# The conditioning sums of the mixing, added by accumulating transfers instead of GpSimd

## The chip, the cores and the metric

The kernel runs on one core of a Trainium2 chip, with one launch. The metric is device time in microseconds, the median over runs. The engines go by the profile's names: TensorE (PE, with PEld for its weight loads), VectorE (DVE), ScalarE (ACT), GpSimd (POOL) and SyncE (SP, which only issues DMAs). Each engine takes its own instructions in the order in which they stand in its queue.

## The reference

One decoder layer, 512 tokens of width 2048, in float32. A conditioning vector `c` gives six vectors by one product with `w_ada` (2048 x 12288): shifts, scales and gates around the mixing (`_m`) and around the MLP (`_f`).

```python
c_act = jax.nn.silu(c)
mod = c_act @ w_ada[l] + b_ada[l]
sh_m, sc_m, gt_m, sh_f, sc_f, gt_f = jnp.split(mod[:, None, :], N_MOD, axis=-1)
h = rmsnorm(x, pre_mix_norm[l]) * (1.0 + sc_m) + sh_m
proj = h @ w_in[l]
o_hg = hgrn2_group(proj[..., :HG_COLS], lb_all[l], hg_norm[l])       # 8 heads
o_gdn = gdn_group(proj[..., HG_COLS:], gdn_conv_w[l], ...)           # 8 heads
y = jnp.concatenate([o_hg, o_gdn], axis=-1) @ w_out[l]
x = x + gt_m * rmsnorm(y, post_mix_norm[l])
h = rmsnorm(x, pre_ffn_norm[l]) * (1.0 + sc_f) + sh_f
y = jnp.square(jax.nn.relu(h @ w_ff1[l])) @ w_ff2[l]
x = x + gt_f * rmsnorm(y, post_ffn_norm[l])
```

The change touches how `sc_f`, `sh_f` and `gt_m` (segments 4, 3 and 2 of `mod`) are summed.

## The kernel before, in words

*Stages.* Until about 288 us the kernel computes `sh_m` and `sc_m`, the normed input and the first projections. From 288 to about 1060 us it runs the **mixing**: 16 heads (8 HGRN2, 8 Gated DeltaNet) whose recurrences are many small dependent steps on VectorE, ScalarE, GpSimd and TensorE, and between them, as filling for TensorE, the projections of the heads to come. From 1060 to about 1280 us follow the output product and the residual, then the MLP until the end.

*Products.* A float32 product is made from three products of split operands (`mm3`). Each weight block of 128x1024 is loaded by SP (`raw`), rounded to its upper part on ScalarE (`wh`, L247), and the rest is taken on VectorE (`wl`, L249). In the mixing `WeightStream.get` hands out such a block for each half of a projection (`pj`), and a raw tile has three buffers.

*Conditioning in the mixing.* Segments 4, 3 and 2 of `w_ada` are read as 3 x 4 x 16 = 192 chunks of 128x512: segment, column block `cb` of 512 columns, row block `r`. A chunk is loaded by SP into an `ada` tile (L469, seven buffers, LOOK = 6 chunks ahead), scaled by ScalarE with the 128 values of `c` for its row block (L487), and added by GpSimd into the sum `aacc` of its column block (L489); the first chunk of a column block is scaled straight into `aacc`. So 180 chunks are added and 12 are not. All 16 row blocks of a column block follow each other, then comes the next column block. Five chunks after a column block's last chunk, `finish` sums the 128 partitions on TensorE (`column_sum`, `pca`) and VectorE puts the result into `sc1f` or `shf`; for segment 2 the bias is added on GpSimd (L1310) and the sum is kept for a product with ones (`pgw`) at the end of the mixing. The sums lie in a pool of six buffers (`part`), which they share with six blocks of the first projections. Segment 5 is summed in the same way, after the mixing (`ada_gtf`, `aaccf`).

*What sets the order.* The orders of TensorE and SP in the mixing are the program's own: a list of threads (`run`) yields in turn, by a clock that counts the matmuls' modelled time. ScalarE, VectorE and GpSimd are put in order by the scheduler of the framework, which also places every wait. Chunks are paced by `on_get`: with each weight block handed out, so many chunks are issued that 192 of them would be through after 84 blocks. Their scaling is put behind the last cast of `wh` (`ws.cast`). On GpSimd the sums stand in one queue with steps of the heads: the powers that make a reciprocal root (L465), the masks (`rsm` L1029, `at` L1098) and small memsets.

*Accumulating transfers* are in the kernel already: in the MLP GpSimd issues DMAs that add a weight quarter from DRAM to a tile in SBUF (`raw` L264, 128x1024), and two near the end add one SBUF tile to another (`add_far`).

Of the kernel before, what the change touches and what calls it, by code (L numbers as in the profile page):

```python
# [13 lines left out]
ALU = mybir.AluOpType  # L14
# [16 lines left out]
NV = 1  # L31
PJ = 3
LOOK = 6
T = 512
D = 2048
KT = D // P
NCH = T // P
NH = 8
# [83 lines left out]
def first_sums(key, t, quarter):  # L122

    c, d, e, f = ((key, q, t) for q in ("11", "22", "12", "n"))
    return ([(c, quarter("11", t)), (d, quarter("22", t)), (e, quarter("12", t))],
            [("pool", e, d, e), ("pool", f, c, e)])
# [168 lines left out]
def hybrid_layer_kernel(  # L295
# [7 lines left out]
    nc = tc.nc  # L303
# [53 lines left out]
    l2, s2 = first_sums(jobs[0][0], 0, jobs[0][2])  # L357
# [5 lines left out]
    def bank(tag, name):  # L363
        return psx.tile([P, T], F32, tag=tag, name=name, bufs={"pj": PJ, "wg": 5 - PJ}.get(tag, 1))

# [17 lines left out]
    ws = WeightStream(nc, wpool, plan, 3, 1, (3, 2, 2, 3))  # L383
# [54 lines left out]

    hH = big.tile([P, KT, T], F32R, tag="hH", name="hH")
    hL = big.tile([P, KT, T], F32R, tag="hL", name="hL")  # L440

# [25 lines left out]
    def ada_load(alloc, seg, cb, r):  # L467
        a = alloc(f"ada{seg}_{cb}_{r}")
        nc.sync.dma_start(out=a, in_=w_ada[2 * len(SLOTS) + (ADA_REST.index(seg) * 4 + cb) * KT + r])  # L469
        return a  # L470
# [6 lines left out]
            else:  # L477
                nc.vector.scalar_tensor_tensor(out=acc, in0=av, scalar=cv, in1=acc, op0=ALU.mult, op1=ALU.add)  # L478

    def ada_pool(a, ncol, r0, nr, acc, first, behind=None):  # L480
        if behind is not None:
            with tc.issue_after(behind):
                return ada_pool(a, ncol, r0, nr, acc, first)
        dst = acc if first else a
        for r in range(nr):
            s = slice(r * ncol, (r + 1) * ncol)
            nc.scalar.activation(out=dst[:, s], in_=a[:, s], func=AF.Copy, scale=c2[:, r0 + r : r0 + r + 1])  # L487
        if not first:
            nc.gpsimd.tensor_tensor(out=acc, in0=a, in1=acc, op=ALU.add)  # L489

    def column_sum(ps, i, a, w, start=True, stop=True):
        for g in range(2):
            s = slice(64 * g, 64 * (g + 1))
            mm(ps[s, i, : w.shape[1]], a[:, s], w, start, stop, cost=0.08)
# [20 lines left out]

    def mt(tag, name, bufs=1, shape=(P, T), dt=F32):
        pool = mixA if tag in MIXA else pools["mix"]
        return pool.tile(list(shape), dt, tag=tag, name=name, bufs=bufs)
# [3 lines left out]
    def conv_silu(u, blk, tag, name, bufs):  # L522
        up = mt("up", f"up{name}", 1, (P, T + 3))
        nc.gpsimd.memset(up[:, :3], 0.0)
        nc.scalar.copy(out=up[:, 3:], in_=u)
        z = mt("z", f"z{name}")
        nc.scalar.activation(out=z, in_=u, func=AF.Copy, scale=convT[:, 72 + blk : 73 + blk])
        for j in range(3):
            nc.vector.scalar_tensor_tensor(out=z, in0=up[:, j : j + T],
                                           scalar=convT[:, j * 24 + blk : j * 24 + blk + 1],  # L530
                                           in1=z, op0=ALU.mult, op1=ALU.add)
        th = mt("th", f"th{name}")
        nc.scalar.activation(out=th, in_=z, func=AF.Tanh, scale=0.5)
        dst = mt(tag, name, bufs)
        nc.vector.scalar_tensor_tensor(out=dst, in0=th, scalar=1.0, in1=z, op0=ALU.add, op1=ALU.mult)
        return dst
# [285 lines left out]
    def ada_thread():  # L822
        nl = 0
        for i, (g, j) in enumerate(SLOTS):
# [26 lines left out]
            if g < NV:  # L851
                ada_vector(t[1], w, nr * j, nr, sums[g][1][:, :w], j == 0)
            else:
                ada_pool(t[1], w, nr * j, nr, sums[g][1], j == 0)
# [436 lines left out]
    def ada_tile(name):  # L1291
        return part_pool.tile([P, T], F32, tag="part", bufs=6, name=name)

    def ada_chunks():
        for seg in (4, 3, 2):
            for cb in range(4):
                for r in range(KT):
                    yield seg, cb, r

    def ada_rest():  # L1300
        todo = list(ada_chunks())
        tiles = {}
        accs_ = {}
        late = []

        def finish(seg, cb, acc):
            if seg == 2:
                bgt = ada_tile(f"bgt{cb}")[0:1, :]
                nc.sync.dma_start(out=bgt, in_=b_ada[:, 2 * D + cb * 512 : 2 * D + (cb + 1) * 512])
                nc.gpsimd.tensor_tensor(out=acc[0:1, :], in0=acc[0:1, :], in1=bgt, op=ALU.add)  # L1310
                gacc.append(acc)
                return
            dst, bias = (sc1f, b_scf) if seg == 4 else (shf, b_shf)
            pc = bank("sh", f"pca{seg}_{cb}").rearrange("p (k n) -> p k n", n=64)
            for k in range(4):
                column_sum(pc, k, acc[:, k * P : (k + 1) * P], ones[:, :64])
            ks = slice(4 * cb, 4 * cb + 4)
            nc.vector.tensor_tensor(out=dst[:, ks], in0=pc[:, 0:4, 0], in1=bias[:, ks], op=ALU.add)
            if seg == 4:
                nc.vector.tensor_tensor(out=dst[:, ks], in0=dst[:, ks], in1=w_pf[:, ks], op=ALU.mult)  # L1320

        for i, (seg, cb, r) in enumerate(todo):
            for s2, c2_, r2 in todo[i : i + LOOK]:
                if (s2, c2_, r2) not in tiles:
                    if r2 == 0:
                        accs_[(s2, c2_)] = ada_tile(f"aacc{s2}_{c2_}")
                    tiles[(s2, c2_, r2)] = ada_load(
                        lambda n: ada_pool_.tile([P, T], F32, tag="ada", bufs=LOOK + 1, name=n),
                        s2, c2_, r2)
            acc = accs_[(seg, cb)]  # L1330
            ada_pool(tiles.pop((seg, cb, r)), 512, r, 1, acc, r == 0, ws.cast)
            if late and i >= late[0][0]:
                finish(*late.pop(0)[1:])
            if r == KT - 1:
                late.append((i + 5, seg, cb, acc))
            yield
        for e in late:
            finish(*e[1:])
# [4 lines left out]
    def ada_gtf():  # L1343
# [16 lines left out]

        for i in range(len(seq) + LOOK + 7):
            if i < len(seq):
                queue.append(ada_load(lambda n: ada_pool_.tile([P, T], F32, tag="ada", bufs=LOOK + 1, name=n),
                                      5, *seq[i]))
            if queue and i >= LOOK:
                cb, r = seq[i - LOOK]
                if r == 0:
                    acc = ada_tile(f"aaccf{cb}")
                ada_pool(queue.pop(0), 512, r, 1, acc, r == 0, ws.cast)
                if r == KT - 1:  # L1370
                    bgt = ada_tile(f"bgf{cb}")[0:1, :]
                    nc.sync.dma_start(out=bgt, in_=b_ada[:, 5 * D + cb * 512 : 5 * D + (cb + 1) * 512])
                    nc.gpsimd.tensor_tensor(out=acc[0:1, :], in0=acc[0:1, :], in1=bgt, op=ALU.add)
                    late.append((i + 6, lambda cb=cb, acc=acc: parts(cb, acc)))
            if late and i >= late[0][0]:
                got = late.pop(0)[1]()
                if got is not None:
                    late.append((i + 8, lambda got=got: finish(*got)))
            yield
        for e in late:  # L1380
            e[1]()

    gsteps = ada_gtf()
    steps = ada_rest()
    pace = {"on": False, "n": 0, "done": 0}
    total = sum(1 for e in plan if e[0][0] == "in1") - 12

    def on_get():
        if not pace["on"]:
            return  # L1390
        pace["n"] += 1
        while pace["done"] * total < pace["n"] * 192:
            pace["done"] += 1
            next(steps, None)

# [136 lines left out]
    with ExitStack() as st:  # L1532
# [41 lines left out]
        for nb in range(1, 4):  # L1574
            ps4 = [bank("pj", f"pout{nb}_{tok}") for tok in range(3)] + [bank("sg", f"pout{nb}_3")]
            n = 8 if nb < 3 else 8 - NLAST
# [494 lines left out]
```

## Time and profile before

| | us |
|---|---|
| median of 3 runs | 2559.31 (2556.16 to 2559.85) |
| profiled execution | 2558.09 |
| its span, first to last instruction | 2556.2 |
| TensorE busy in the span | 2427.4 (95%) |
| VectorE busy | 1959.9 (77%) |
| ScalarE busy | 1264.3 (49%) |
| GpSimd busy | 992.9 (39%) |
| mean granted TensorE clock | 0.983 |

The profile is of one execution; times within it count from the first instruction. "Busy" is the union of an engine's instructions, and a matmul's end is modelled. A row of the waits reads: who waited, at which line, on what; us in total, times, longest. A row of a tile reads: line, engine, operation, out<-in, count; shortest/median/longest ns, first and last start. A row of the timeline: start, us, engine, line, operation, and in brackets the idle time before it and what ended it. The page's "PEclk" is the clock that the throttle granted to TensorE, as a share of full speed.

### The profile page before, as it was taken

The page shows a single profiled execution, that of the slowest core. Times are in us where ns is not written, and L with a number is a line of the kernel's source. Part 1 is how long each engine was busy: PE and PEld are TensorE (multiplying, and loading weights), DVE is VectorE, ACT ScalarE, POOL GpSimd, SP SyncE. Part 2 cuts the span into 40 slices and gives each one's busy share as a digit, 9 for nine tenths or more (in the row PEclk, how much of TensorE's full clock was granted, in tenths as well). Part 3 has the DMA queues.
Part 4 walks back from the last instruction along what each step waited for, and adds up shares of the span by engine and source line. Part 5 has one row for each costly group of instructions (what it writes and reads, how often), then busy time and mean ns, then how long its engine had stood idle before and what let it go on. Part 6 is the DMA issues. An engine that isn't in the chain of part 4 may idle for free.

```text
span 2556.2 us, 39334 instructions
## 1 busy us (share of the span) xinstructions
PE 2427.4 (95%) x14763; PEld 2065.9 (81%) x14763; DVE 1959.9 (77%) x2615; ACT 1264.3 (49%) x2012; POOL 992.9 (39%) x720
## 2 busy tenths in 40 slices
PE   5889999998999899999899999999999999999997
PEld 3667777777777778778779999999998888888886
DVE  7997887768595866654687777878788788888887
ACT  5554444444444443465555565656665433333333
POOL 4561244545454541186231222212235244244343
PEclk8999999999999999999999999999999999999999
DMA  8762434444445442476458887888889988988876
GB/s 312 256 211 78 130 121 132 138 156 131 155 147 158 139 146 75 136 264 226 165 173 252 242 273 238 245 253 237 273 249 301 287 252 246 287 258 244 265 211 192
DMA packets 202899, 527.18 MB, mean 206 GB/s; under 512 B 19026, under 2 KB 23492, under 8 KB 202068
## 3 DMA queue, kind: packets, MB, share of 16 engines
q1 hardware_dynamic: 183792, 457.49, 51.6%
q0 software_dynamic: 18144, 66.07, 14.1%
q8 instruction: 116, 1.90, 0.3%
q10 hardware_dynamic: 772, 1.11, 0.1%
q14 instruction: 75, 0.61, 0.1%
HBM read 460.08 MB, written 63.46 MB: 205 GB/s over the span
## 4 chain that ended last, share of the span: by engine, by line
PE 63%; DVE 6%; ACT 2%; issue 2%; POOL 2%; DMA 1%; POOLq 0%; DVEq 0%; SPq 0%; ACTq 0%
PE qx L369 13%; PE px L369 13%; PE pj L369 10%; PE py L369 7%; PE qy L369 6%; PE pout L369 4%; PE pz L369 3%; PE qz L369 3%; DVE wl L249 1%; POOL aaccf L489 1%; PE pa L369 1%; DMA raw<-in_w_ff_dram 0%; DVE uc L1070 0%; PE p L369 0%; DVE utmp L1068 0%
## 5 line engine op out<-in xcount | busy, mean ns | idle before, releaser
L249 DVE TENSOR_TENSOR wl<-raw,wh 128x1024 fp32r<-128x1024 f32 x457 | 701.8, 1541 | 215.2 <-ACT wh L247 214.0
L247 ACT CAST wh<-raw 128x1024 fp32r<-128x1024 f32 x463 | 485.4, 1049 | 625.8 <-PE pj L369 172.1
L489 POOL TENSOR_TENSOR aacc<-ada,aacc 128x512 f32<-128x512 f32 x180 | 270.4, 1503 | 257.3 <-ACT ada L487 249.9
L369 PE MATMUL pj<-hH,wh 128*128 128x512 f32 x768 | 325.6, 424 | 0.0
L369 PE MATMUL pj<-hH,wl 128*128 128x512 f32 x768 | 305.4, 398 | 3.6 <-DVE wl L249 3.6
L369 PE MATMUL pj<-hL,wh 128*128 128x512 f32 x768 | 303.9, 396 | 0.0
L264 POOL DMA_DIRECT2D raw<-in_w_ff_dram x92 | 80.9, 879 | 527.8 <-DVE wl L249 425.3
L269 POOL TENSOR_TENSOR raw<-raw,raw 128x1024 f32<-128x1024 f32 x54 | 161.4, 2989 | 126.5 <-DVE wl L249 68.2
L369 PEld LDWEIGHTS pj<-hH,wl 128*128 128x128 f32 x768 | 146.3, 191 | 38.8 <-DVE wl L249 5.7
L369 PEld LDWEIGHTS pj<-hH,wh 128*128 128x128 f32 x768 | 147.4, 192 | 29.0
L369 PEld LDWEIGHTS pj<-hL,wh 128*128 128x128 f32 x768 | 147.5, 192 | 23.6
L487 ACT ACTIVATE ada<-ada,c 128x512 f32<-128x512 f32 x240 | 160.6, 715 | 0.7 <-DMA ada<-in_w_ada_dram 0.7
L369 PE MATMUL px<-hA,wl 128*128 128x256 f32 x480 | 135.9, 283 | 2.3 <-DVE wl L249 2.3
L249 DVE TENSOR_TENSOR w<-raw,w 128x1024 fp32r<-128x1024 f32 x59 | 116.8, 1992 | 26.5 <-ACT w L247 26.5
L369 PE MATMUL px<-hB,wh 128*128 128x256 f32 x480 | 135.8, 283 | 0.0
L369 PE MATMUL px<-hA,wh 128*128 128x256 f32 x480 | 135.8, 283 | 0.0
L489 POOL TENSOR_TENSOR aaccf<-ada,aaccf 128x512 f32<-128x512 f32 x60 | 99.1, 1652 | 43.0 <-ACT ada L487 38.1
L478 DVE SCALAR_TENSOR_TENSOR asum<-adas,c,asum 128x256 f32<-128x256 f32 (+1 forms) x150 | 105.8, 716 | 2.7 <-DMA adas<-in_w_ada_dram 0.2
L369 PE MATMUL pout<-wh,oH 128*128 128x512 f32 x256 | 101.9, 400 | 3.7 <-ACT wh L247 2.2
L247 ACT CAST w<-raw 128x1024 fp32r<-128x1024 f32 x59 | 61.9, 1049 | 87.6 <-PE qx L369 43.6
L369 PE MATMUL pout<-wl,oH 128*128 128x512 f32 x256 | 100.6, 394 | 1.1 <-DVE wl L249 1.1
L369 PE MATMUL pout<-wh,oL 128*128 128x512 f32 x256 | 100.8, 394 | 0.6 <-DVE oL L1505 0.6
(565 smaller groups left out, 6740.2 us busy)
## 6 DMA issues: line engine op xcount, KB each, us to landing
raw<-in_w_ff_dram SPq DMA_DIRECT2D x233, 512.0 KB, 4.6
raw<-in_w_in_dram SPq DMA_DIRECT2D x128, 512.0 KB, 3.7
ada<-in_w_ada_dram SPq DMA_DIRECT2D x256, 256.0 KB, 3.4
raw<-in_w_ff_dram POOLq DMA_DIRECT2D x92, 512.0 KB, 5.9
adas<-in_w_ada_dram SPq DMA_DIRECT2D x128, 256.0 KB, 4.6
gd<-Y SPq DMA_DIRECT2D x30, 1024.0 KB
hA<-gd SPq DMA_DIRECT2D x47, 512.0 KB, 8.2
hB<-gd SPq DMA_DIRECT2D x47, 512.0 KB, 8.1
```

The source lines that it names most:

```text
L247: self.cast = self.nc.scalar.copy(out=h, in_=raw).ins
L249: eng.tensor_tensor(out=lo, in0=raw, in1=h.bitcast(F32), op=ALU.subtract)
L264: self.nc.gpsimd.dma_start(out=o, in_=src[0], accum_op=ALU.add)
L269: eng.tensor_tensor(out=o, in0=self.raw[src[-1]], in1=self.raw[src[0]], op=ALU.add)
L369: nc.tensor.matmul(ps, lhsT=lhsT, rhs=rhs, start=start, stop=stop, skip_group_check=chain)
L478: nc.vector.scalar_tensor_tensor(out=acc, in0=av, scalar=cv, in1=acc, op0=ALU.mult, op1=ALU.add)
L487: nc.scalar.activation(out=dst[:, s], in_=a[:, s], func=AF.Copy, scale=c2[:, r0 + r : r0 + r + 1])
L489: nc.gpsimd.tensor_tensor(out=acc, in0=a, in1=acc, op=ALU.add)
```

## The change

Five things change, all of them in the mixing. The 180 sums are no longer a GpSimd instruction with two inputs: GpSimd issues a DMA that reads the scaled chunk from SBUF and adds it to `aacc` in SBUF (`accum_op=ALU.add`, through the new argument `far`). The row blocks become the outer loop and the four column blocks the inner one, so that four sums are open at a time and two transfers into the same sum lie four chunks apart. Chunks are loaded 4 ahead (LOOK1) instead of 6, with seven buffers as before. A sum's tile is taken when its first chunk is scaled instead of when it is loaded. The pace goes from 192 to 198. Segment 5 keeps its GpSimd sums. Lines behind the change have numbers that are higher by 1 to 5 in the changed kernel (L469 is L470, L489 is L494, the transfer is L492, L465 is L466).

```diff
+LOOK1 = 4
...
-    def ada_pool(a, ncol, r0, nr, acc, first, behind=None):
+    def ada_pool(a, ncol, r0, nr, acc, first, behind=None, far=False):
         if behind is not None:
             with tc.issue_after(behind):
-                return ada_pool(a, ncol, r0, nr, acc, first)
+                return ada_pool(a, ncol, r0, nr, acc, first, None, far)
         dst = acc if first else a
         for r in range(nr):
             s = slice(r * ncol, (r + 1) * ncol)
             nc.scalar.activation(out=dst[:, s], in_=a[:, s], func=AF.Copy, scale=c2[:, r0 + r : r0 + r + 1])
-        if not first:
+        if first:
+            return
+        if far:
+            nc.gpsimd.dma_start(out=acc, in_=a, accum_op=ALU.add)
+        else:
             nc.gpsimd.tensor_tensor(out=acc, in0=a, in1=acc, op=ALU.add)
...
         for seg in (4, 3, 2):
-            for cb in range(4):
-                for r in range(KT):
+            for r in range(KT):
+                for cb in range(4):
                     yield seg, cb, r
...
-            for s2, c2_, r2 in todo[i : i + LOOK]:
+            for s2, c2_, r2 in todo[i : i + LOOK1]:
                 if (s2, c2_, r2) not in tiles:
-                    if r2 == 0:
-                        accs_[(s2, c2_)] = ada_tile(f"aacc{s2}_{c2_}")
                     tiles[(s2, c2_, r2)] = ada_load(
                         lambda n: ada_pool_.tile([P, T], F32, tag="ada", bufs=LOOK + 1, name=n),
                         s2, c2_, r2)
+            if r == 0:
+                accs_[(seg, cb)] = ada_tile(f"aacc{seg}_{cb}")
             acc = accs_[(seg, cb)]
-            ada_pool(tiles.pop((seg, cb, r)), 512, r, 1, acc, r == 0, ws.cast)
+            ada_pool(tiles.pop((seg, cb, r)), 512, r, 1, acc, r == 0, ws.cast, True)
...
-        while pace["done"] * total < pace["n"] * 192:
+        while pace["done"] * total < pace["n"] * 198:
```

## The prediction

> **What bounds the kernel now.** I read the busy time by stretch first, for the mixing, in which the changed code runs (288 us to 1060 us of the span), then the waits of TensorE there, then what those waits stand behind.
>
> ```profile
> core 0: us, PE busy (x) PEld busy (x) DVE busy (x) ACT busy (x) POOL busy (x), PEclk, DMA share, GB/s
> 288.00:1060.00 772.00, 729.97 (x4673) 583.98 (x4672) 549.02 (x1068) 356.08 (x734) 330.69 (x259) 0.98 0.42 136
> 288.00:968.50 680.50, 639.47 (x4106) 512.65 (x4104) 493.68 (x944) 322.18 (x668) 325.63 (x254) 0.98 0.44 143
> 968.50:1050.00 81.50, 81.34 (x507) 65.55 (x507) 48.20 (x108) 24.32 (x47) 5.05 (x6) 1.00 0.25 78
> 1280.00:1900.00 620.00, 614.02 (x5000) 606.69 (x5000) 489.18 (x469) 371.64 (x508) 151.40 (x98) 1.00 0.82 245
> ```
>
> TensorE is the bound: it is busy for 730.0 of 772 us. What can be won in the mixing is its idle time, 42.0 us, of which 41.0 us lie before 968.5 us; behind that, where the last of the GpSimd sums is done, it idles 0.2 us in 81.5 us. Its waits there (the first three and the last of 15 rows):
>
> ```profile
> PE p L369 <- DVE S L1182: 10.6, 6, 2.8
> PE py L369 <- DVE Ud L1086: 7.4, 3, 3.8
> PE pj L369 <- DVE wl L249: 3.6, 5, 1.2
> ...
> PE pa L369 <- DVE utmp L1068: 0.2, 1, 0.2
> ```
>
> All 15 rows name VectorE, and they add up to 41.9 us. So TensorE waits for nothing but VectorE, though VectorE itself is busy for only 71% (549.0 of 772). The tiles show why it is late: the same instruction has two durations.
>
> ```profile
> L489 POOL TENSOR_TENSOR aacc<-ada,aacc x180: 1252/1352/2473, 297.0 to 963.5; 128x512 f32<-128x512 f32 x180
> L1236 DVE TENSOR_TENSOR KS<-KS,tot x36: 411/419/2757, 320.5 to 949.6; 128x256 f32<-128x256 f32 x36
> L1236 DVE TENSOR_TENSOR KS<-KS,tot x4: 416/418/420, 1036.1 to 1051.9; 128x256 f32<-128x256 f32 x4
> L249 DVE TENSOR_TENSOR wl<-raw,wh x84: 1206/1225/2321, 296.4 to 961.1; 128x1024 fp32r<-128x1024 f32 x84
> L249 DVE TENSOR_TENSOR wl<-raw,wh x12: 1183/1218/1226, 972.9 to 1044.7; 128x1024 fp32r<-128x1024 f32 x12
> L1236 DVE TENSOR_TENSOR KS<-KS,tot 128x256 f32<-128x256 f32 x36 | 27.7, 769 | 0.0
> L249 DVE TENSOR_TENSOR wl<-raw,wh 128x1024 fp32r<-128x1024 f32 x84 | 114.1, 1358 | 41.1 <-ACT wh L247 40.6
> ```
>
> The update of KS takes 0.41 us at best and 2.76 us at worst while the sums run, and 0.42 us in all four cases after them (minimum/median/maximum). On the mean it is 0.77 us, so its 36 instructions lose 36 x (769 - 411) ns = 12.9 us; the split of the weights loses 84 x (1358 - 1206) ns = 12.8 us. With the same subtraction for every VectorE instruction of the mixing (its duration less the lower quartile of its shape), 112.7 us are lost, and 101.6 us of them in 114 instructions that lie mostly beside one of the 180 sums of L489. The longest stall shows it (VectorE, then GpSimd, then TensorE):
>
> ```profile
> 875.56 1.16 DVE L1068 TENSOR_TENSOR utmp<-X,uc 128x12 f32<-128x12 f32 x1
> 876.75 2.43 DVE L1070 TENSOR_TENSOR uc<-uc,utmp 128x12 f32<-128x12 f32 x1
> 879.21 0.17 DVE L1068 TENSOR_TENSOR utmp<-X,uc 128x8 f32<-128x8 f32 x1
> 872.96 3.73 POOL L489 TENSOR_TENSOR aacc<-ada,aacc 128x512 f32<-128x512 f32 x2 [2.21 <-ACT ada L487]
> 877.89 2.61 POOL L489 TENSOR_TENSOR aacc<-ada,aacc 128x512 f32<-128x512 f32 x2
> 881.45 0.80 PE L369 MATMUL py<-Ud,Ap 64*64 64x64 f32 x10 [3.78 <-DVE Ud L1086]
> ```
>
> Instructions on 12 columns take 1.16 and 2.43 us beside GpSimd sums, where one on 8 takes 0.17 us; behind their chain TensorE stands for 3.78 us.
>
> **The change part by part.**
>
> *180 sums leave GpSimd, 180 accumulating transfers come.* GpSimd loses 270.4 us (180 x 1503 ns) and gets 180 issues. The mixing has no such issue; the feed-forward part has:
>
> ```profile
> L264 POOL DMA_DIRECT2D raw<-in_w_ff_dram x92: 860/878/1092, 1310.6 to 2496.3; - x92
> 1333.83 3.31 DVE L249 TENSOR_TENSOR wl<-raw,wh 128x1024 fp32r<-128x1024 f32 x1
> 1338.81 2.35 DVE L249 TENSOR_TENSOR wl<-raw,wh 128x1024 fp32r<-128x1024 f32 x2
> 1333.66 2.41 POOL L269 TENSOR_TENSOR raw<-raw,raw 128x1024 f32<-128x1024 f32 x1 [1.16 <-DVE wl L249]
> 1340.38 0.88 POOL L264 DMA_DIRECT2D raw<-in_w_ff_dram  x1 [2.06 <-DVE wl L249]
> ```
>
> 180 x 0.88 = 158 us, so GpSimd is freer by 112 us, which alone is worth nothing. What counts is VectorE: beside a GpSimd sum the weight split took 3.31 us, beside an issue two of them took 2.35 us together. I take it that an issue holds VectorE up by nothing. Bounds: nothing, or as long per microsecond as a sum does (158/270 = 58% of the loss stays).
>
> What TensorE gets of it, stall by stall: I followed each of the 26 stalls over 0.3 us (40.8 us together) back over what released it to the last matmul, added up what VectorE lost on that way, and credited the smaller of loss and stall. In the one above 7.5 us were lost for a stall of 3.8. In all it gives 29.7 us of the 40.8; in four stalls (9.4 us together) the way back names no VectorE instruction, and I credit nothing. GpSimd keeps its other sums (10 of the 112.7 us lost), so I take 27 us. Bounds: 58% kept, 11 us; all waits gone, 41.9 us.
>
> *The clock.* After stalls TensorE runs at half clock (a stall, then the first, the fifth and the last of seven such stretches):
>
> ```profile
> 323.48 0.80 PE L369 MATMUL p<-S,kT 128*128 128x128 f32 x2 [2.13 <-DVE S L1182]
> ...
> 323.30:330.00 6.70, 6.52 (x30) 5.32 (x31) 6.60 (x16) 0.48 (x3) 0.99 (x1) 0.50 0.45 157
> ...
> 616.90:620.20 3.30, 3.30 (x10) 2.82 (x11) 3.06 (x12) 1.29 (x2) 0.00 (x0) 0.50 0.05 19
> ...
> 879.70:886.40 6.70, 4.95 (x25) 4.06 (x26) 6.53 (x13) 0.00 (x0) 2.20 (x2) 0.50 0.33 100
> ```
>
> Two last 6.7 us and five 3.3 us, 29.9 us, which cost half of that, 15 us. Five of them, 23 us long, follow stalls that I credit; I take 10 us for the clock (bounds 0 and 15). The Trainium skill, "TensorE: Matmul & The Clock Gate", section "What's actually happening", says that the clock is halved after an idle window of about 3.4 us; by that only the stall of 3.78 us would count, half of 6.7 us, and the sum would be 7 us smaller. The trace doesn't agree: the stretch at 323.3 us follows a stall of 2.1 us, so the measurement decides.
>
> *Column blocks in turns.* The sums of one segment now end together, and so do their column sums on TensorE. TensorE before (pca: column sums; aacc: a column block's sum), then after:
>
> ```order
> L369 MATMUL pj1280_3348<-hH_95,wl39_3352 128x512
> L369 MATMUL pca4_0_3538<-ones_74,aacc4_0_2800 64x64 [waits DVE_49,Pool_49]
> L369 MATMUL pca4_0_3538<-ones_74,aacc4_0_2800 64x64 x7
> L369 MATMUL pj256_3523<-hH_95,wh40_3433 128x512
> L369 MATMUL pj256_3523<-hL_96,wh40_3433 128x512
> ```
>
> ```order
> L370 MATMUL pj2432_4983<-hH_95,wl59_4987 128x512
> L370 MATMUL pca4_1_5124<-ones_74,aacc4_1_2812 64x64 [waits DMASW1_49,DVE_49]
> L370 MATMUL pca4_1_5124<-ones_74,aacc4_1_2812 64x64 x7
> L370 MATMUL pca4_2_5139<-ones_74,aacc4_2_2816 64x64 [waits DMASW2_49,DVE_49]
> L370 MATMUL pca4_2_5139<-ones_74,aacc4_2_2816 64x64 x7
> L370 MATMUL pca4_3_5154<-ones_74,aacc4_3_2861 64x64 [waits DMASW3_49,DVE_49]
> L370 MATMUL pca4_3_5154<-ones_74,aacc4_3_2861 64x64 x7
> ```
>
> Three stand in a row and share one bank, so each waits until VectorE has read the one before; VectorE's queue holds a weight split (1.2 us) and two smaller instructions between. That is three such turns in all (two here, one in the next segment), 0.3 to 2 us each: I take 4 us lost (bounds 1 and 6).
>
> *The queues.* GpSimd before (L465 and L1029 are steps of the heads), then after:
>
> ```order
> L465 TENSOR_TENSOR gsc1_2997<-gsc1_2997,mhalf_78 128x4 [waits DVE_49]
> L1029 TENSOR_TENSOR rsm1_3072<-stril_83,gsc1_2997 128x512 [waits DVE_49]
> L489 TENSOR_TENSOR aacc4_0_2800<-ada4_0_7_2818,aacc4_0_2800 128x512 [waits Activation_49,Pool_49]
> L489 TENSOR_TENSOR aacc4_0_2800<-ada4_0_8_2863,aacc4_0_2800 128x512 [waits Activation_49,Pool_49]
> L489 TENSOR_TENSOR aacc4_0_2800<-ada4_0_9_2867,aacc4_0_2800 128x512 [waits Activation_49,Pool_49]
> ```
>
> ```order
> L466 TENSOR_TENSOR gsc1_2997<-gsc1_2997,mhalf_78 128x4 [waits DVE_49,Pool_49]
> L529 MEMSET upqT2_3335 128x3 [waits DVE_49,Activation_49]
> L1034 TENSOR_TENSOR rsm1_3068<-stril_83,gsc1_2997 128x512 [waits DVE_49]
> L492 DMA aacc4_0_2808<-ada4_0_2_2921 128x512 [waits DMASW0_49,Activation_49]
> L492 DMA aacc4_1_2812<-ada4_1_2_2925 128x512 [waits DMASW1_49,Activation_49]
> ```
>
> Each transfer now waits on GpSimd's queue for the landing of the one four back (DMASW), with the heads' steps queued behind; and SP's load of a chunk waits for the landing of the one that held its buffer, with the weight loads queued behind. The rows for both:
>
> ```profile
> DMA to landing us min/median/max: 5.2/6.7/11.3
> DMA to landing us min/median/max: 2.5/3.4/5.9
> L487 ACT ACTIVATE ada<-ada,c x240: 704/714/733, 296.3 to 1210.2; 128x512 f32<-128x512 f32 x120
> SPq L469 <- POOL aacc L489: 194.5, 142, 9.2
> POOL rqs L465 <- DVE rqs L464: 29.1, 6, 20.6
> L369 PE MATMUL pgw<-aacc,ones x8: 592/593/595, 1051.9 to 1054.9; 128*128 128x512 f32 x8
> q0 software_dynamic: 18144, 66.07, 14.1%
> ```
>
> (First GpSimd's accumulating transfers, twice as large, then the chunk loads.) A sum starts every 3.5 us ((963.5 - 297.0)/191 for 192 chunks), so four back is 14 us back, over the 6.7 us of a landing and the 11.3 us of the worst; and a load goes out four chunks after its buffer's transfer was queued, before two after its sum. So I take 2 us lost (bounds 0 and the rival's price). The last sums have from 963.5 to 1051.9 us until they are read, 88 us. The transfers move 47.2 MB; at queue 0's rate (14.1% of the span for 66.07 MB) that adds 257 us of the DMA engines to 680 us, a share of 0.44 + 0.38 = 0.82, as in the feed-forward stretch above, where TensorE is busy for 99%. The faster pace (198 for 192) moves work by 3%: nothing.
>
> Sum: -27 - 10 + 4 + 2 = -31 us. The profiled execution took 2558.1 us, 1.2 us under the median, so 2527 us there and 2528 us for the median.
>
> **The rivals.**
> 1. *The stream of chunks becomes the bound (slower).* Seven buffers at 3.5 us give 24.5 us a round; load 3.4, scaling 0.7 and issue 0.9 leave 19.5 us from issue to landing. Beyond it SP holds back the weights, 192/7 = 27 us for each further microsecond, so at 20.6 us the gain is eaten and 22 us give about 2597 us. For it: GpSimd's one wait of 20.6 us, during which nothing behind it is issued. Against: the landing would have to be three times the median of a transfer twice its size. The Trainium skill, "DMA: Bandwidth & Descriptors", section "Two DMAs through the same engine are not ordered", asks for this wait on the earlier transfer's semaphore before a dependent one is issued; no run here shows what the wait costs on GpSimd's queue.
> 2. *Half the gain.* Issues hold VectorE up as sums do, or ScalarE or another VectorE chain stands right behind: 0.42 x 37 - 6 = 10 us, 2550 us. Against: the 2.35 us above.
> 3. *No change:* the stalls move, since VectorE's instructions stand in another order; 2554 to 2564 us. Against: the 0.2 us of idle time after the sums' end, though the last head has less beside it.
> 4. *All of it:* 41.9 + 15 - 6 = 51 us, 2508 us.
>
> **How the numbers follow.** A measurement of this kernel tells 0.2% (5 us) from no change. My forecast (2514 to 2540 us) 0.56, rival 4 0.06, rival 2 0.21, rival 3 0.08, rival 1 0.09. Faster 0.83, same 0.08, slower 0.09. The range goes from rival 4 to just above rival 2: 2508 to 2552 us.
>
> **What would show it.** After: KS of L1236 at about 0.42 us at its maximum save beside `rsm` and `at`; VectorE's busy time in the mixing lower by about 100 us; TensorE idle under 20 us there; half-clock stretches two or fewer; GpSimd issues of 0.9 us with landings under 10 us. I am wrong if VectorE's instructions stay long beside the issues, or if SP waits for landings and `pj` for `raw`.

## The result, and the profile after

The changed kernel takes 2517.17 us (2513.86 to 2518.13, 5 runs) where the kernel before took 2559.31 us on the same chip: a ratio of 0.9838, with a 95% interval of 0.9824 to 0.9852, or 42 us less. Its profiled execution has a span of 2516.4 us against 2556.2. The prediction, 2528 us with a range of 2508 to 2552, had the direction and the mechanism; 11 us more were won than it said.

The mixing now ends, with the first `pgw`, at 1011 us instead of 1051.8. Windows, before (its mixing up to that point) and then after; the columns are those of the prediction's first fence:

```profile
288.00:1051.80 763.80, 722.61 (x4635) 579.57 (x4634) 542.46 (x1053) 347.90 (x716) 330.69 (x259) 0.98 0.42 136
```

```profile
288.00:1011.00 723.00, 711.52 (x4644) 574.58 (x4642) 443.50 (x1056) 348.54 (x717) 218.90 (x259) 0.99 0.83 209
1240.00:1860.00 620.00, 612.80 (x4987) 605.93 (x4985) 488.22 (x468) 371.90 (x506) 150.34 (x97) 0.99 0.83 245
591.10:597.90 6.80, 5.45 (x15) 4.51 (x16) 6.28 (x20) 3.34 (x5) 0.84 (x3) 0.50 0.74 190
700.40:703.80 3.40, 3.40 (x11) 2.82 (x12) 3.40 (x7) 2.52 (x6) 1.07 (x2) 0.50 0.26 37
```

The mixing is 40.8 us shorter: TensorE's idle time went from 41.2 to 11.5 us, and its busy time fell by 11.1 us for the same matmuls, mostly because two stretches at half clock are left (10.2 us, the last two rows) where there were seven (30.7 us by the clock's records; the prediction's windows cut them to 29.9). VectorE does the same instructions in 99 us less. The feed-forward part takes what it took (612.8 us of 620, 40 us earlier). The tiles and lines that the prediction was read from, after:

```profile
L492 POOL DMA_DIRECT2D aacc<-ada x180: 850/887/1473, 304.1 to 908.0; - x180
L1241 DVE TENSOR_TENSOR KS<-KS,tot 128x256 f32<-128x256 f32 x39 | 17.4, 446 | 0.0
L250 DVE TENSOR_TENSOR wl<-raw,wh x98: 1206/1224/1234, 287.4 to 1010.8; 128x1024 fp32r<-128x1024 f32 x98
DMA to landing us min/median/max: 3.3/7.1/10.9
q0 software_dynamic: 44064, 113.27, 24.9%
```

The split of the weights has one duration now, 1.21 to 1.23 us in 98 cases, where it reached 2.32; KS takes 0.446 us on the mean where it took 0.769. TensorE's waits in the mixing, after (all but three rows of 0.3 to 0.5 us):

```profile
PE pog L381 <- DVE uc L1075: 3.4, 1, 3.4
PE hpo L370 <- DVE hat L1281: 2.6, 3, 1.9
PE hp L370 <- DVE hS L1273: 1.6, 1, 1.6
PE pca L370 <- DVE sc1f L1323: 1.4, 2, 1.1
PE pca L370 <- DVE shf L1323: 0.9, 1, 0.9
...
PE pca L370 <- DMA aacc<-ada: 0.2, 1, 0.2
```

All but the last still name VectorE. The waits of `p`, `py` and `pj`, the first three rows of before, are gone or down to half a microsecond.

### The profile page after: what moved, and what is told of

Read it like the earlier page. It is cut to its first block, busy times and chain, and to the rows that moved or that the text cites. A ratio compares the mean times of both kernels' runs of the same rounds, so it can differ in the third digit from the quotient of the medians.

```text
span 2516.4 us, 39399 instructions
## 1 busy us (share of the span) xinstructions
PE 2415.9 (96%) x14763; PEld 2060.6 (82%) x14763; DVE 1864.0 (74%) x2615; ACT 1265.8 (50%) x2012; POOL 880.5 (35%) x720
## 4 chain that ended last, share of the span: by engine, by line
PE 48%; DVE 2%; issue 1%; DMA 1%; ACT 1%; POOL 0%; POOLq 0%; DVEq 0%; SPq 0%; ACTq 0%
PE px L370 14%; PE qx L370 13%; PE py L370 7%; PE qy L370 6%; PE pz L370 3%; PE qz L370 3%; PE pout L370 1%; DMA raw<-in_w_ff_dram 1%; DVE wl L250 1%; DVE h2t L1638 0%; ACT tail L1929 0%; DVE Y L1945 0%; DVE hsum L1740 0%; DVE hB L1646 0%; POOL hB L1747 0%
## 5 line engine op out<-in xcount | busy, mean ns | idle before, releaser
L492 POOL DMA_DIRECT2D aacc<-ada x180 | 159.2, 981 | 321.9 <-ACT ada L488 231.6
L494 POOL TENSOR_TENSOR aaccf<-ada,aaccf 128x512 f32<-128x512 f32 x60 | 98.6, 1643 | 41.0 <-ACT ada L488 36.0
```

Source lines behind the costliest of these rows:

```text
L492: nc.gpsimd.dma_start(out=acc, in_=a, accum_op=ALU.add)
```

## The experiments

The theory: GpSimd's sums read SBUF and so hold up VectorE's two-input instructions; VectorE comes late; TensorE waits and loses its clock behind the waits. The rivals: the new order or pace brought the gain; it was GpSimd's queue, where the heads' steps stood behind the sums; and, on the side of the costs, that the transfers take something back. Each kernel was timed beside the kernel before on its own chip; ratios are to that, and their intervals reach 0.0013 to 0.0019 to either side.

**Only the sums back on GpSimd** (order, pace and loads as changed; TensorE's, ScalarE's and SP's orders are the same row for row):

```diff
-            ada_pool(tiles.pop((seg, cb, r)), 512, r, 1, acc, r == 0, ws.cast, True)
+            ada_pool(tiles.pop((seg, cb, r)), 512, r, 1, acc, r == 0, ws.cast)
```

> The changed kernel with its new order, pace and loads, but with the 180 sums as GpSimd instructions again. TensorE's, ScalarE's and SP's orders are the changed kernel's. Theory (the sums on GpSimd hold up VectorE's two-input instructions): VectorE is busy for about 540 us again from 288 us to the end of the mixing, KS reaches over 1.5 us, TensorE idles about 40 us there, and the time is 2554 to 2564 us. Rival (the order, the pace or the later loads brought the gain): 2517 to 2540 us, with VectorE's instructions beside the sums as short as in the changed kernel or with the stalls elsewhere.

Measured: 2570.82 us, ratio 1.0063 (1.005 to 1.0077). Its mixing in the windows:

```profile
288.00:1063.50 775.50, 727.69 (x4638) 583.11 (x4637) 549.18 (x1055) 347.11 (x716) 326.47 (x259) 0.97 0.41 134
```

And its waits of column sums:

```profile
PE pca L370 <- DVE utmp L1073: 5.8, 1, 5.8
PE pca L370 <- DVE sc1f L1323: 3.3, 2, 1.8
```

VectorE is at 549 us again and TensorE idles for 47.8 us. So the operation alone is worth 2.2%, and the order with the pace and the later loads is a cost: 16 us here, above what was expected, with 9.1 us of waits for `pca`, which the kernel before did not have.

**The kernel before without the sums:**

```diff
-        if not first:
+        if not first and add:
             nc.gpsimd.tensor_tensor(out=acc, in0=a, in1=acc, op=ALU.add)
```

> The kernel before with the 180 sums left out: chunks are loaded and scaled, but only the first of each column block counts, so the conditioning of the residual and the MLP is not the reference's. No transfers, old order, old pace. It shows what the sums cost as they were, and by its distance to the changed kernel what the transfers cost. Theory: VectorE's loss falls to about 10 us, TensorE idles 8 to 12 us in the mixing, time 2508 to 2518 us; the transfers cost the changed kernel at most 5 us. Rival (the transfers cost TensorE something that the trace of the changed kernel hides: waits on SP, ScalarE, DMA traffic): over 8 us below the changed kernel, under 2509 us. Rival (the gain is not from the sums' going): 2540 us or more.

Measured: 2501.46 us, ratio 0.9789 (0.9776 to 0.9802). Its mixing:

```profile
288.00:992.80 704.80, 704.17 (x4635) 570.07 (x4634) 445.04 (x1053) 348.53 (x716) 63.19 (x79) 1.00 0.45 147
```

TensorE idles for 0.6 us and never runs at half clock. The sums cost the whole of its idle time, and the changed kernel pays 12 to 16 us for what replaced them (0.0049 to 0.0062 of the time before, by its two timings). That is the rival of "over 8 us", not the "at most 5" that I had held.

**Dummy work on GpSimd, first try.** Two additions of a spare tile to itself, or four fills of it, behind each issue in the program's text:

```diff
             nc.gpsimd.dma_start(out=acc, in_=a, accum_op=ALU.add)
+            for _ in range(2):
+                nc.gpsimd.tensor_tensor(out=spare, in0=spare, in1=spare, op=ALU.add)
```

> The changed kernel, and behind each of the 180 issues GpSimd adds a spare 128x256 tile to itself, twice (two inputs from SBUF, about 0.7 us each, some 250 us in all, near the 270 us of the sums). Nobody waits for the results. Theory (a GpSimd instruction that reads SBUF holds up VectorE): the loss comes back, VectorE is busy for 80 to 120 us more in the mixing, KS reaches over 1 us, time 2540 to 2570 us. Rival (what counted is that the heads' steps no longer stand behind the sums on GpSimd's queue): slower too, but equally so with the writes of the next kernel. Rival (the sums cost by their wait for ScalarE and by the chunks' order): 2515 to 2522 us.

> As the kernel with the dummy reads, but GpSimd fills the spare 128x256 tile with zeros four times behind each issue (no input from SBUF; about 0.3 us each, some 220 us in all). GpSimd is as busy as in the kernel before. Theory: VectorE loses nothing to them, its busy time in the mixing is within 15 us of the changed kernel's 443.5, time 2515 to 2525 us. Rival (GpSimd's queue): within 5 us of the kernel with the dummy reads. Rival (any GpSimd work on SBUF holds VectorE up): 2540 us or more.

Measured: 2693.38 us (ratio 1.0543, 1.0528 to 1.0557) with the reads and 2581.75 us (1.0104, 1.009 to 1.0117) with the writes, both above what was expected. Neither tests the theory, and the reads' row shows why:

```profile
L494 POOL TENSOR_TENSOR spare<-spare x360: 606/613/1675, 13.9 to 358.1; 128x256 f32<-128x256 f32 x180
```

Nothing tied the dummies to the transfers, so the scheduler put them at the start, ahead of the sums of `sh_m` and `sc_m` that the first projections wait for; the mixing came later as a whole.

**Dummy work, tied to its place.** The same, but queued behind its issue:

```diff
-            nc.gpsimd.dma_start(out=acc, in_=a, accum_op=ALU.add)
+            d = nc.gpsimd.dma_start(out=acc, in_=a, accum_op=ALU.add)
+            with tc.issue_after(d.ins):
+                for _ in range(2):
+                    nc.gpsimd.tensor_tensor(out=spare, in0=spare, in1=spare, op=ALU.add)
```

> The dummy reads again, this time each pair queued behind its issue on GpSimd, so that they run among the heads' steps in the mixing and not at the start: two additions of a spare 128x256 tile to itself behind each of the 180 transfers, about 1.2 us a pair, 220 us in all. GpSimd has more to do than in the kernel before (issues and additions). Theory (a GpSimd instruction that reads SBUF holds up VectorE): VectorE loses 80 us or more in the mixing, KS reaches over 0.9 us, time at least 25 us above the changed kernel. Rival (only the queue counts): VectorE's loss stays near 11 us, and the time is within 5 us of the kernel with the writes.

> The same place on GpSimd's queue and about the same time, but only writes: the spare 128x256 tile is filled with zeros four times behind each issue (0.31 us each, 1.25 us together). Theory: VectorE's loss stays near 11 us; what is lost against the changed kernel is the heads' steps standing behind more work, 5 to 20 us. The distance to the kernel with the reads, 20 us or more, is the price of the reads alone. Rival (any GpSimd work holds VectorE up): VectorE loses 80 us or more here as well.

Measured: reads 2584.31 us (1.011, 1.009 to 1.0129), writes 2526.49 us (0.9881, 0.9864 to 0.9899). The mixing of each in the windows, first with the reads, then with the writes:

```profile
288.00:1072.90 784.90, 729.00 (x4628) 583.59 (x4624) 542.09 (x1053) 346.33 (x716) 481.83 (x619) 0.97 0.77 192
```

```profile
288.00:1018.70 730.70, 711.75 (x4640) 574.47 (x4638) 443.06 (x1055) 348.22 (x716) 438.29 (x979) 0.99 0.82 207
```

And the same place in the timelines of both, GpSimd and then VectorE, in the same order:

```profile
319.29 1.66 POOL L495 TENSOR_TENSOR spare<-spare 128x256 f32<-128x256 f32 x2
321.51 2.47 POOL L495 TENSOR_TENSOR spare<-spare 128x256 f32<-128x256 f32 x2
319.50 0.98 DVE L1244 TENSOR_TENSOR QP<-QP,tot 128x256 f32<-128x256 f32 x1
320.40 0.83 DVE L1246 TENSOR_TENSOR KS<-KS,tot 128x256 f32<-128x256 f32 x1
321.16 2.35 DVE L250 TENSOR_TENSOR wl<-raw,wh 128x1024 fp32r<-128x1024 f32 x1
```

```profile
319.45 0.97 POOL L495 MEMSET spare<- 128x256 f32 x2
321.59 2.50 POOL L495 MEMSET spare<- 128x256 f32 x6
319.68 0.41 DVE L1244 TENSOR_TENSOR QP<-QP,tot 128x256 f32<-128x256 f32 x1
320.01 0.41 DVE L1246 TENSOR_TENSOR KS<-KS,tot 128x256 f32<-128x256 f32 x1
320.35 1.21 DVE L250 TENSOR_TENSOR wl<-raw,wh 128x1024 fp32r<-128x1024 f32 x1
```

The update of QP and that of KS take 0.98 and 0.83 us beside additions, and 0.41 us each beside fills; the weight split takes 2.35 us beside additions, and 1.21 us where it lies between two groups of fills. Over the mixing the update of KS takes 0.83 us at the median with the reads (37 cases) and 0.42 us, median and maximum, with the fills (39 cases). GpSimd is busy for 438 us with the fills, 108 more than in the kernel before, and VectorE loses nothing (443.1 us against 443.5). With the reads it is at 542.1, where it was before the change. The 58 us between the two are the price of the additions over the fills. GpSimd's queue is not what parts them: the additions keep GpSimd busy 43.5 us longer, but VectorE waits for the heads' powers alike, 51.6 us with the reads and 50.6 with the fills. Against the changed kernel the fills cost 8 to 11 us (0.9881 against its two ratios), which is the price of the longer queue. An addition reads SBUF and also computes, and no run here parts the two; that the reading does it fits what the Trainium skill states ("SBUF — State Buffer", section "Who interferes with whom"): a VectorE instruction with two SBUF inputs contends with a GpSimd instruction that reads SBUF, not with one that only writes it. The two traces agree.

**Why 12 to 16 us are left.** First the transfers made narrow, then taken away in the new order, with the changed kernel again on the chip of the latter:

```diff
-            nc.gpsimd.dma_start(out=acc, in_=a, accum_op=ALU.add)
+            nc.gpsimd.dma_start(out=acc[:, :16], in_=a[:, :16], accum_op=ALU.add)
```

> The changed kernel with transfers of the first 16 of 512 columns only: the same 180 issues in the same places, hardly any bytes, so that they land soon and none waits for one before it. The conditioning then lacks the sums of the other columns. In the changed kernel no transfer starts before the landing of the third one before it, and the heads' powers stand behind such waits on GpSimd's queue. If these waits (or the bytes) are what is left between the changed kernel and the one without sums, this kernel comes within 4 us of the one without sums: a ratio to the kernel before of 0.978 to 0.981. If the issues themselves are it (0.88 us each on GpSimd's queue) or the order of the chunks, it stays within 3 us of the changed kernel: 0.982 to 0.985.

```diff
-        if far:
-            nc.gpsimd.dma_start(out=acc, in_=a, accum_op=ALU.add)
-        else:
+        if not far:
```

> The changed kernel with its order, pace and loads, but without the 180 transfers (only the first chunk of each column block counts, so the conditioning is not the reference's). With the kernel without sums in the old order it was 0.979 of the kernel before, with narrow transfers in the new order 0.982. If the new order (column sums in a row, chunks of four sums in turns) costs what is left, this kernel is at 0.981 to 0.983 too; if the issues on GpSimd's queue and their waits cost it, it is at 0.977 to 0.980, TensorE idles under 3 us in the mixing and shows at most one half-clock stretch.

> The changed kernel itself, once more on the chip of these runs, to compare the small differences with. Every theory expects 0.982 to 0.986 of the kernel before.

Measured: narrow 2512.24 us (0.982, 0.9803 to 0.9838); none 2509.45 us (0.9819, 0.9806 to 0.9833); the changed kernel again 2516.68 us (0.9851, 0.9838 to 0.9864). The mixing without transfers:

```profile
288.00:1004.00 716.00, 708.27 (x4629) 571.75 (x4623) 445.01 (x1053) 346.85 (x716) 60.75 (x79) 1.00 0.44 145
```

Its waits of the column sums, and the timeline at the longest of them:

```profile
PE pca L370 <- DVE shf L1321: 2.4, 1, 2.4
PE pca L370 <- DVE sc1f L1321: 1.4, 2, 1.2
```

```profile
711.32 1.12 PE L370 MATMUL pca<-ones,aacc 128*64 128x64 f32 x16 [2.41 <-DVE shf L1321]
712.96 0.63 PE L370 MATMUL pj<-hL,wh 128*128 128x512 f32 x1
```

So the leftover has two halves. One is the order, with the pace and the loads: 0.9819 against 0.9789, 7.7 us, without any transfer. The column sums in a row wait for 3.8 us there, and with the longest wait TensorE's clock is halved for 6.8 us (a `pj` matmul takes 0.63 us there, 0.39 before it). The other is the transfers: 2516.68 against 2509.45 on the same chip, 7.2 us (5 us by the changed kernel's first ratio, 0.9838). That the narrow ones come out as none at all (0.982 and 0.9819) says that the 180 issues cost nothing that can be measured, and that the wide transfers do, by their bytes or by their longer landings. By itself the narrow kernel spoke for the issues or the order, as I had put its numbers; only the kernel without transfers tells which. Its interval touches that of the changed kernel, so of this split the sign is firmer than the size. The two halves don't lie in the same places either: in the changed kernel the column sums wait for 2.5 us (three rows of `pca` above), and neither of its half-clock stretches follows them.

Where the transfers' part arises shows at the longest wait of the changed kernel, 3.4 us of `pog` (GpSimd, then VectorE, then TensorE; the wait runs from 589.05 to 592.45 us, and the clock is halved from 591.1 us):

```profile
587.82 0.85 POOL L492 DMA_DIRECT2D aacc<-ada  x1 [1.71 <-DMA aacc<-ada]
589.43 0.85 POOL L492 DMA_DIRECT2D aacc<-ada  x1 [0.76 <-issue]
590.00 1.35 POOL L466 TENSOR_TENSOR rsg<-rsg,mhalf 128x4 f32<-128x4 f32 x1
587.86 0.17 DVE L465 TENSOR_SCALAR rsg<-rsg 128x4 f32<-128x4 f32 x1
591.38 0.16 DVE L992 TENSOR_TENSOR rsg<-rsg,rqs 128x4 f32<-128x4 f32 x1 [2.88 <-POOL rsg L466]
592.45 0.88 PE L381 MATMUL pog<-ident,at 128*128 128x128 f32 x3 [3.40 <-DVE uc L1075]
```

The input of the power of `rsg` is ready at 588.0 us, but on GpSimd's queue two transfers stand ahead of the power. Each of the two starts 0.3 us after the landing of the third transfer before it (those landed at 587.5 and 589.1 us), though the second one's row calls its wait "issue". VectorE stands behind that with all it has queued. Over the mixing VectorE waits for such powers for 41.6 us in the changed kernel (14.3, 11.0, 10.6 and 5.7 for `rqs`, `rsg`, `gsc` and `rsh`; 36.8 in its second trace), 28.5 without transfers.

**Each chunk an eighth of a weight block apart, and column sums apart.** Chunks handed out evenly instead of two or three with each weight block; then also the four column sums of a segment two chunks apart (`on_block` stands in `project` behind each `mm3`, and does what `on_get` did):

```diff
+                on_block()
...
-        while pace["done"] * total < pace["n"] * 198:
+        while pace["done"] * total * 8 < pace["n"] * 198:
...
-                late.append((i + 5, seg, cb, acc))
+                late.append((i + 4 + cb, seg, cb, acc))
```

> The changed kernel with the chunks handed out evenly: the pace is counted with each eighth of a weight block instead of with each block, so that chunks are loaded one at a time instead of two or three together. All transfers stay. Theory (transfers in bunches wait for the third one before them, and the heads' powers wait behind them): the waits of transfers on landings fall from 42 us to under 15, TensorE idles under 6 us in the mixing, and the time is 5 to 12 us below the changed kernel, a ratio to the kernel before of 0.979 to 0.982. Rival (issues, not waits): 0.983 to 0.985. Rival (ScalarE and SP in another order make new stalls): above 0.985.

> A candidate for a better version: the even pace of the kernel before the last, and the four column sums of a segment put two chunks apart on TensorE (4, 5, 6 and 7 chunks behind the last row block of their column block) instead of in a row. If the row of column sums costs 2 to 3 us, the waits of pca fall under 0.5 us, and the time is 1 to 4 us below that of the even pace alone, a ratio to the kernel before of 0.979 to 0.982. If other waits take their place: 0.982 to 0.985.

Measured: even pace alone 2511 us (0.9823, 0.9804 to 0.9842); both 2507.23 us (0.981, 0.9797 to 0.9824). The mixing of the one with both, and two of its waits:

```profile
288.00:997.90 709.90, 705.31 (x4629) 570.00 (x4624) 443.55 (x1053) 348.06 (x716) 221.81 (x259) 1.00 0.84 213
```

```profile
PE hpo L370 <- DVE hat L1282: 2.1, 4, 1.0
POOL aacc L492 <- DMA aacc<-ada: 31.6, 17, 5.9
```

No wait of `pca` is left, TensorE idles for 4.6 us, and the mixing has no half-clock stretch. This kernel beats the changed one: 9.5 us under it on the same chip, with intervals apart. Against the even pace alone nothing is shown, since the intervals overlap; so do those of the even pace alone and the changed kernel, and its 0.9823 lies between what the theory (up to 0.982) and the rival (from 0.983) asked for. The reason I gave for the even pace fell: the transfers waited 32.8 us for landings with it, not under 15, and TensorE idled for 7.7 us, not under 6. The changed kernel's own two traces have 41.7 and 22.8 us of such waits, so their sum says little about the time. What the kernel with both gained beyond the waits of `pca`, and whether that is more than a lucky placement, stays open.

**The old order with transfers:**

```diff
-            for r in range(KT):
-                for cb in range(4):
+            for cb in range(4):
+                for r in range(KT):
```

> The changed kernel with the old order of the chunks: all 16 row blocks of a column block, then the next column block, so that each transfer adds to the sum of the one just before it and must wait for its landing. A lone transfer lands 3.3 us after its issue at best; a chunk is due every 3.35 us. Theory (GpSimd's queue waits for each landing, with the heads' powers behind it, and SP waits for the chunks' buffers): one chunk every 3.6 to 5 us at best, so the stream of 180 ends 45 to 300 us later than in the changed kernel, the mixing becomes longer by that, and the time is 2560 to 2800 us. Rival (the turns were not needed, landings are hidden): within 10 us of the changed kernel.

Measured: 2842.31 us, ratio 1.1126 (1.1111 to 1.1141), worse than the top of what I expected by 42 us. Its mixing, and five of its waits:

```profile
288.00:1335.90 1047.90, 762.34 (x4635) 612.31 (x4635) 440.83 (x1053) 352.19 (x717) 221.68 (x259) 0.85 0.59 144
```

```profile
POOL aacc L492 <- DMA aacc<-ada: 433.2, 106, 8.2
DVE rsg L992 <- POOL rsg L466: 98.4, 7, 26.7
DVE gsc L1023 <- POOL gsc L466: 88.3, 7, 21.1
PE pca L370 <- DMA aacc<-ada: 67.4, 5, 21.3
PE pj L370 <- DVE wl L250: 12.4, 3, 7.4
```

GpSimd waits 433 us for landings, the powers wait behind, up to 26.7 us, and TensorE idles for 286 us with a clock of 0.85. VectorE's instructions are as short as ever (440.8 us). So the stream of chunks has become the bound, as the prediction's first rival has it, and the turns keep that away. But the weights are not what TensorE lacks: `pj` waits for 12.4 us, while the column sums wait 67.4 us for the transfers themselves, and most of the rest names VectorE, which stands behind the powers.

## Why the prediction was right, point by point

*What bounds.* Right: TensorE waited for VectorE, and VectorE was late because of GpSimd's sums. The kernel with only the sums back shows it with one thing changed, and the tied dummies show that it is the additions beside VectorE and not their place in the queue.

*An issue holds VectorE up by nothing.* Right: with the prediction's own subtraction VectorE's loss is 10.9 us after (112.7 before), 0.3 of it beside transfers. Rival 2 is out.

*Stalls, -27 us.* Too small. With the sums away TensorE's idle time went from 41.2 to 0.6 us: every stall was theirs. What failed was crediting nothing to the four stalls whose way back named no VectorE instruction (9.4 us), and to others only what VectorE lost since the last matmul; its lateness probably went back further, which I haven't shown. Rival 4's size was the right one here.

*The clock, -10 us.* Also too small: without the sums no half-clock stretch is left of 30.7 us, worth the upper bound of 15. The changed kernel keeps 10.2 us of them, so 10 was what came out, partly by luck: all 15 us were won, and 5 lost again behind the waits of `pog` and `hpo`.

*Column sums in a row, +4 us.* The place was right, but 7.7 us were measured for order, pace and loads together, above the bound of 6. Without transfers the waits came to 3.8 us, as said, and I had not charged the clock that the longest of them costs. In the changed kernel itself they came to 2.5 us and cost no clock.

*The queues, +2 us.* Mis-sized: 7.2 us, or 5 by the first ratio. The step that failed is "four back is 14 us back". Chunks come two or three at once, and no transfer of the changed kernel started sooner than 0.25 us after the landing of the third before it, so landings of 7 us do reach the queue. SP's waits for the chunks' buffers, the other half of that step, held up no `pj`.

*Traffic.* Right but for the worst landing: a share of 0.83 over the mixing, landings of 7.1 us at the median and 10.9 at worst, where 6.7 and under 10 were said.

So the sum has two errors of opposite sign, which by luck partly cancel: some 56 us (41 of stalls and 15 of clock) instead of 37 were in the sums, and some 15 instead of 6 went to what replaced them; -42 came out instead of -31. Of the things that would show it, KS has one long case inside the mixing, 1.51 us beside the bias addition on GpSimd (L1315), which I had not named; the rest came as said, landings aside.

## What to carry to other kernels

When VectorE's same instruction has two durations, look at what GpSimd reads in the meantime; a sum on GpSimd is not free because GpSimd is idle, and moving it to accumulating transfers gave back most of what it cost (42 of 54 us). Such transfers need several independent sums in turns, since each must wait for the landing of the one before into the same bytes (4.2 us at the median, alone), and whatever stands behind them on GpSimd's queue waits along. When several short column sums come due together, give each its own time: without the transfers one wait of 2.4 us cost TensorE twice, once as a wait and once as clock.

## What the hardware showed that was not expected

- At most three accumulating transfers were in flight. Of the 177 that have three before them none started sooner than 0.25 us after the landing of the third one back, and 59 started within half a microsecond of it; the program asks only for the fourth. Of the narrow transfers, of 8 KB instead of 256, only one waited for a landing, 4.1 us; it started 0.31 us after the landing of the third one back, and none started sooner. By this one case it isn't the bytes. What sets the limit no run tells.
- A transfer of 16 columns lands 4.4 us after its issue at the median, one of 512 columns 7.1, and one of 512 columns 4.2 in the old order, where 170 of 180 start after the landing of the one before. The rest of the 7.1 goes with the other transfers in flight and with busier DMA engines (a share of 0.83 against 0.59); no run parts the two.
- TensorE's clock was halved with waits of 2.4 us (column sums, without transfers) and of 1.9 us (`hpo`, in the changed kernel), for 6.8 and 3.4 us. By the idle window of about 3.4 us that the Trainium skill gives ("TensorE: Matmul & The Clock Gate", section "What's actually happening") neither would have halved it; the traces don't agree.
- The clock's records show where a wait costs clock. In the trace of the kernel before and in that after, the nine half-clock stretches of the mixing begin on one grid of 3.41 us within each trace and last one or two of its steps. Each begins after a step in which TensorE idled for 1.87 us or more, and no step at full clock with 1.83 us of idle time or less was followed by one. In the other runs the border lies there too, between 1.78 and 1.87 us, but for one stretch in the old order behind 1.39 us. So a wait costs clock when enough of it falls into one step: in the kernel before, a wait of 2.56 us that began at 496.6 us, shared by two steps, cost none.
